# Output projection of three token blocks moved between in-projection blocks, operands split beside their weights, on one Trainium2 core

## The chip, the cores and the metric

The kernel runs on one core of a Trainium2 chip. The metric is the device time of one execution in microseconds (us). TensorE is called PE (its weight loads PEld), VectorE DVE, ScalarE ACT; SyncE (SP) issues every DMA of this kernel from one queue, in order. PE, DVE, ACT and SP each work through their own list of instructions in order; a framework writes these lists ahead of time, by a priority that follows the order of the Python program, and puts in the waits.

## The reference

One decoder layer over 2048 tokens of width 1024, in float32. What is computed, cut to its frame:

```
h = rmsnorm(x, norm1_w);  proj = h @ w_in                    # 1024 -> 3840
o_hg = hgrn2(first 2048 columns)                             # 4 heads of 128, gated linear recurrence
o_rw = rwkv7(last 1792 columns, shifted by a token and mixed)  # 8 heads of 64
x = x + concat(o_hg, o_rw) @ w_out
u = rmsnorm(x, norm2_w) @ w_up                               # 1024 -> 5632
u = causal depthwise conv of width 3 + bias;  gate, val = split(u)
x = x + (silu(gate) * val) @ w_down                          # 2816 -> 1024
out = rmsnorm(x, final_norm_w)
```

## The kernel before, in words

Tokens lie in four blocks (`nb` or `b`, 0 to 3) of 512. Every large product is made of three 128x512 matmuls a step (`mm3`, L194): each operand is split into a rounded high part, cast by ACT, and a low part, subtracted by DVE (`split`, L165, `split_to`, L161).

**Stage one** (`phase1`, L200) runs three generators side by side. `dense` (L343) is a list of jobs: for each block an "A" job (load four 128-token tiles of `x`, two at a time; square sum on ACT, scaling on DVE; transpose on PE, with ACT and DVE writing `hh` and `hl`), then 30 "P" jobs, each one 128-column strip of the in-projection: 24 matmuls into a `pj` bank, weights in `wraw` tiles (256 KB). At the end of the list stands "O" for block 0, `out_block` (L307): its output projection with the residual. `rw_stream` and `hg_stream` are the two recurrences, chains of small matmuls (`rw`, `hg` banks), DVE and ACT steps; the RWKV chain goes twice per pair of heads through DRAM (`Ed` to `E`, then `Td` to `TTs` and `TZ`). Each step of a recurrence lets `dense` proceed by 550 ns of matmuls (`fill`). There are two `pj` banks. Results go to DRAM: `oT` (recurrence outputs, transposed), `x1d` (residual rows), `h2d` (normalised, transposed rows for the next product).

**Output stage** (L926): for blocks 1, 2 and 3, one after another, load and split all eight `oT` tiles, load four `x` tiles, then for each half of the columns eight steps of twelve matmuls (`wacc`), add the residual, store `x1d`, and for blocks 1 and 2 normalise, transpose and store `h2d`. Then `build(0)`.

**Up-projection** (`half`, L984, for token halves 0 and 1): one level of a Strassen-like scheme, seven products in place of eight. `build(h)` (L898) makes its seven token operands: for each of four row groups `kk` it loads four 256 KB tiles of `h2d` (blocks 2h and 2h+1), forms sums with four DVE subtractions and splits seven tiles into `Bh`, `Bl`. For each of 22 feature blocks `fb`, weight tiles `uraw` are loaded, combined and split, and 84 matmuls go to `ua`, `ub`, `ud`; convolution and gate follow, and `gd` is stored to DRAM. Block 3 is normalised inside half 0 at `fb` 2 and 4 (`norm_last`, L968).

**Down-projection** (L1073): for each block load and split all 22 `gd` tiles (`graw`), then for each half of the columns 22 steps of a weight tile (`wdraw`) and twelve matmuls (`dacc`); residual, final norm, store.

Of the kernel before, what the change touches and what calls it, by code (L numbers as in the profile page):

```python
# [7 lines left out]
F32 = mybir.dt.float32  # L8
F32R = mybir.dt.float32r
BF16 = mybir.dt.bfloat16  # L10
# [8 lines left out]
P = 128  # L19
# [41 lines left out]
def tile_layer(ctx, tc, consts, x, norm1_w, w_in, hg_lb_logits, hg_norm_w, rw_shift_mu, rw_w0, rw_w2,  # L61
# [10 lines left out]

    cst = cp.tile([P, C_W], F32, name="cst")
    dma(cst, consts)
    ident = cst[:, C_ID:C_ID + P]
# [97 lines left out]
    def rstd(pool, xt, name, sqt="nsq"):  # L173

        sq = pool.tile([P, D], BF16, tag=sqt, name="nsq", bufs=1)
# [6 lines left out]
    def norm_transpose(pool, xt, nm, psum, evict, sqt="nsq"):  # L182

        n = len(xt)
        for t_ in xt:
            V.tensor_scalar_mul(t_, t_, rstd(pool, t_, "nst", sqt))
# [13 lines left out]
    def phase1(c1):  # L200
# [106 lines left out]
        def out_block(nb):  # L307

            for k in range(KD):
                raw = wp.tile([P, BLK], F32, tag="wraw", name="oraw", bufs=3)  # L310
                dma(raw, oT[nb][k * P:(k + 1) * P, :])
                split_to(hh[:, k, :], hl[:, k, :], raw)
            for i2 in range(2):
                xt = []
                for q in range(2):
                    t_ = wp.tile([P, D], F32, tag="xt", name="xt", bufs=2)
                    t0 = nb * BLK + (i2 * 2 + q) * P
                    dma(t_, x[0, t0:t0 + P, :])
                    xt.append(t_)
                for dh in range(2):  # L320
                    accs = [bank("pj") for _ in range(2)]
                    for k in range(KD):
                        raw = wp.tile([P, 512], F32, tag="wraw", name="woraw", bufs=3)
                        dma(raw, w_out[0, k * P:(k + 1) * P, dh * 512:dh * 512 + 512])
                        wh, wl = split(wp, raw, [P, 512], "w", 4)
                        for q in range(2):
# [3 lines left out]
                    for q in range(2):  # L330
                        V.tensor_add(xt[q][:, dh * 512:dh * 512 + 512], accs[q], xt[q][:, dh * 512:dh * 512 + 512])
                for q in range(2):
                    r0 = (i2 * 2 + q) * P
                    dma(x1d[nb][r0:r0 + P, :], xt[q])

                def evict(k, tp, w):
                    t_ = wp.tile([P, 256], F32, tag="h2", name="h2", bufs=2)
                    act(t_, tp, AF.Copy, scale=w)
                    dma(h2d[nb][k * P:(k + 1) * P, i2 * 256:i2 * 256 + 256], t_)

                yield from norm_transpose(wp, xt, "n2", lambda: bank("pj"), evict)
# [524 lines left out]
    if "1" in stages:  # L866
        with ExitStack() as c1:
            phase1(c1)
# [264 lines left out]
```

## Time and profile before

| | us |
|---|---|
| median of 3 runs (range) | 3017.43 (3015.49 to 3018.39) |
| the profiled execution | 3016.65 |
| its span, first to last instruction | 3014.9 |
| PE busy in it | 2779.6 (92%) |
| DVE busy | 1973.2 (65%) |
| ACT busy | 1423.3 (47%) |
| first in-projection matmul | at 41.0 |
| first `wacc` matmul | at 1402.2 |
| first `ua` matmul | at 1609.3 |
| first `dacc` matmul | at 2521.8 |

"Granted clock" or PEclk is the share of its full clock that PE was given. A row of waits reads: who waited, for whom, us in total, how often, longest. In a group, the mean of one instruction in ns stands ahead of the second bar, and behind it the idle time ahead of the instructions with what ended it. Durations of matmuls overlap, since they are pipelined; the distance of their starts is what each costs.

### The profile page before, as it was taken

How to read it: one execution, taken by the hardware profiler on the slowest of the kernel's cores; microseconds unless marked ns; L12 is line 12 of the kernel's file. 1: busy time of each engine (PE TensorE's matmuls, PEld its weight loads, DVE VectorE, ACT ScalarE, POOL GpSimd, SP SyncE). 2: the span in 40 equal slices, each digit the busy share in tenths (PEclk: the TensorE clock that was granted, in tenths of full speed). 3: DMA queues.
4: the chain of work that ended last, by engine and by line, in shares of the span. 5: the costliest groups of instructions: out<-in, count | busy, mean ns of one | idle time of the engine just before them, and what ended most of it. 6: DMA issues, size and time to landing. Idle time of an engine off the chain costs nothing.

```text
span 3014.9 us, 47475 instructions
## 1 busy us (share of the span) xinstructions
PE 2779.6 (92%) x18323; PEld 2201.0 (73%) x18323; DVE 1973.2 (65%) x3889; ACT 1423.3 (47%) x2390; POOL 0.2 (0%) x4
## 2 busy tenths in 40 slices
PE   5999899989998999987678899998999995999998
PEld 4777677767776777666557788886888874888887
DVE  4778668776877586853545687778777774445343
ACT  4545553655354454543434655555555543334332
POOL 0000000000000000000000000000000000000000
PEclk9999899999998999988889999998999997999999
DMA  3222222222313222246653322223222216456442
GB/s 119 71 66 67 76 77 73 67 80 64 89 55 79 74 65 76 68 127 197 210 174 108 121 83 84 84 88 101 84 84 84 84 56 213 158 173 223 143 154 97
DMA packets 361295, 316.47 MB, mean 105 GB/s; under 512 B 61303, under 2 KB 278637, under 8 KB 361069
## 3 DMA queue, kind: packets, MB, share of 16 engines
q1 hardware_dynamic: 361069, 313.44, 33.8%
q8 instruction: 144, 2.36, 0.3%
q14 instruction: 82, 0.67, 0.1%
HBM read 250.44 MB, written 62.91 MB: 104 GB/s over the span
## 4 chain that ended last, share of the span: by engine, by line
PE 79%; DVE 7%; ACT 6%; DMA 5%; issue 2%; SPq 1%; DVEq 0%; ACTq 0%
PE pj L196 8%; PE pj L197 7%; PE pj L198 7%; PE ua L196 5%; PE ua L197 5%; PE ua L198 5%; PE dacc L196 5%; PE dacc L197 5%; PE dacc L198 5%; PE ud L198 2%; PE ud L196 2%; PE ud L197 2%; PE hg L750 2%; PE ub L196 1%; PE ub L198 1%
## 5 line engine op out<-in xcount | busy, mean ns | idle before, releaser
L196 PE MATMUL pj<-hh,wh 128*128 128x512 f32 x960 | 420.1, 438 | 1.5 <-ACT wh L169 0.9
L197 PE MATMUL pj<-hl,wh 128*128 128x512 f32 x960 | 382.3, 398 | 0.0
L198 PE MATMUL pj<-hh,wl 128*128 128x512 f32 x960 | 380.6, 396 | 0.6 <-DVE wl L170 0.6
L169 ACT CAST wh<-wraw 128x512 fp32r<-128x512 f32 x240 | 146.6, 618 | 347.5 <-PE pj L197 295.4
L196 PE MATMUL dacc<-wdh,ggh 128*128 128x512 f32 x704 | 274.4, 391 | 36.9 <-ACT wdh L169 36.9
L196 PE MATMUL ua<-Bh,uwh 128*128 128x512 f32 x704 | 276.9, 393 | 19.6 <-ACT m L108 9.9
L197 PE MATMUL ua<-Bl,uwh 128*128 128x512 f32 x704 | 276.0, 392 | 9.6 <-DVE Bl L163 9.6
L198 PE MATMUL ua<-Bh,uwl 128*128 128x512 f32 x704 | 275.2, 391 | 0.0
L197 PE MATMUL dacc<-wdl,ggh 128*128 128x512 f32 x704 | 275.0, 391 | 0.0
L198 PE MATMUL dacc<-wdh,ggl 128*128 128x512 f32 x704 | 274.8, 390 | 0.0
L170 DVE TENSOR_TENSOR wl<-wraw,wh 128x512 fp32r<-128x512 f32 x240 | 162.4, 684 | 146.3 <-ACT wh L169 144.8
L170 DVE TENSOR_TENSOR wdl<-wdraw,wdh 128x512 fp32r<-128x512 f32 x176 | 120.9, 689 | 184.9 <-ACT wdh L169 184.8
L169 ACT CAST uwh<-uraw 128x512 fp32r<-128x512 f32 x220 | 136.1, 619 | 203.7 <-PE ua L197 86.1
L196 PEld LDWEIGHTS pj<-hh,wh 128*128 128x128 f32 x960 | 180.9, 188 | 64.6 <-issue 20.1
L197 PEld LDWEIGHTS pj<-hl,wh 128*128 128x128 f32 x960 | 181.4, 189 | 40.8 <-issue 12.0
L198 PEld LDWEIGHTS pj<-hh,wl 128*128 128x128 f32 x960 | 180.8, 188 | 41.5 <-DVE wl L170 1.4
L169 ACT CAST wdh<-wdraw 128x512 fp32r<-128x512 f32 x176 | 109.0, 619 | 204.9 <-PE dacc L198 178.0
L170 DVE TENSOR_TENSOR uwl<-uraw,uwh 128x512 fp32r<-128x512 f32 x220 | 147.3, 685 | 86.0 <-ACT uwh L169 84.8
L196 PEld LDWEIGHTS dacc<-wdh,ggh 128*128 128x128 f32 x704 | 132.7, 189 | 65.4 <-ACT wdh L169 38.2
L196 PEld LDWEIGHTS ua<-Bh,uwh 128*128 128x128 f32 x704 | 133.1, 189 | 51.4 <-ACT m L108 12.7
L197 PEld LDWEIGHTS ua<-Bl,uwh 128*128 128x128 f32 x704 | 133.3, 189 | 37.7 <-DVE Bl L163 10.3
L198 PEld LDWEIGHTS ua<-Bh,uwl 128*128 128x128 f32 x704 | 133.1, 189 | 27.9 <-DVE uwl L170 0.2
(263 smaller groups left out, 5622.5 us busy)
## 6 DMA issues: line engine op xcount, KB each, us to landing
wraw<-in_w_in_dram SPq DMA_DIRECT2D x240, 256.0 KB
uraw<-in_w_up_dram SPq DMA_DIRECT2D x176, 256.0 KB
wdraw<-in_w_down_dram SPq DMA_DIRECT2D x176, 256.0 KB
gd<-y SPq DMA_DIRECT2D x88, 256.0 KB
graw<-gd SPq DMA_DIRECT2D x88, 256.0 KB
woraw<-in_w_out_dram SPq DMA_DIRECT2D x80, 256.0 KB
xt<-in_x_dram SPq DMA_DIRECT2D x32, 512.0 KB
xt<-x1d SPq DMA_DIRECT2D x20, 512.0 KB
```

The costliest lines, as they stand in the source:

```text
L169: S.copy(hi, src)
L170: V.tensor_sub(lo, src, hi.bitcast(F32))
L196: TE.matmul(acc, lh, rh, start=first, stop=False, skip_group_check=skip)
L197: TE.matmul(acc, lh, rl, start=False, stop=False, skip_group_check=skip)
L198: TE.matmul(acc, ll, rh, start=False, stop=last, skip_group_check=skip)
L750: TE.matmul(lp[e * 64:e * 64 + 64, b * 64:b * 64 + 64], kt[:, t0:t0 + 64], qt[:, t0:t0 + 64], start=True, stop=True, tile_position=(0, e * ...
```

## The change

The job list of stage one becomes longer. "O" for blocks 0, 1 and 2 now stand in it: O(0) ahead of A(2), O(1) ahead of A(3), O(2) at the end. A new job "L" loads the next block's four `x` tiles and scales them, twenty jobs into the block before, so that "A" only transposes, now all four tiles into one bank. A new job "N" normalises a block's `x1d` rows, read back from DRAM, and writes `h2d`: N(0) and N(1) ten jobs into blocks 2 and 3, N(2) at the end. `out_block` loads and splits each `oT` tile beside the weight tile of the same step and takes residual rows in halves. The tags of scratch tiles are merged (`wraw` with four buffers now also holds squares, residual halves and `h2`).

In the output stage block 3 alone is left, its `oT` tiles also split beside the weights. The sums of the Strassen operands are formed by `sums`, stored to DRAM (`Ts`) and read back by `build`, which now goes operand by operand through six buffers; those of half 1 are formed at `fb` 6 to 9 of half 0. In the down-projection `graw` tiles are loaded and split beside `wdraw` tiles. The first block's `x` tiles are loaded ahead of the small parameters.

```diff
+    def load_rows(src, r0):
+        t_ = xp_.tile([P, D], F32, tag="xt", name="xt", bufs=4)
+        dma(t_, src[r0:r0 + P, :])
+        return t_
+
     cst = cp.tile([P, C_W], F32, name="cst")
+    first = [load_rows(x[0], i * P) for i in range(2)]
     dma(cst, consts)
+    first += [load_rows(x[0], i * P) for i in range(2, 4)]
...
         def out_block(nb):
 
-            for k in range(KD):
-                raw = wp.tile([P, BLK], F32, tag="wraw", name="oraw", bufs=3)
-                dma(raw, oT[nb][k * P:(k + 1) * P, :])
-                split_to(hh[:, k, :], hl[:, k, :], raw)
             for i2 in range(2):
...
                     for k in range(KD):
-                        raw = wp.tile([P, 512], F32, tag="wraw", name="woraw", bufs=3)
+                        if i2 == 0 and dh == 0:
+                            raw = wp.tile([P, BLK], F32, tag="wraw", name="oraw", bufs=4)
+                            dma(raw, oT[nb][k * P:(k + 1) * P, :])
+                            split_to(hh[:, k, :], hl[:, k, :], raw)
+                        raw = wp.tile([P, 512], F32, tag="wraw", name="woraw", bufs=4)
...
+        def normed(src, r0, xt=None):
+
+            xt = xt or [load_rows(src, r0 + i * P) for i in range(4)]
+            for t_ in xt:
+                V.tensor_scalar_mul(t_, t_, rstd(wp, t_, "nst", "wraw", 4))
+            return xt
...
-            jobs = []
+            jobs = [("L", 0)]
             for nb in range(NBLK):
+                if nb >= 2:
+                    jobs.append(("O", nb - 2))
                 jobs.append(("A", nb))
...
-            jobs.append(("O", 0))
+            jobs += [("O", 2), ("N", 2)]
+
+            at = [i for i, jb in enumerate(jobs) if jb[0] == "A"]
+            for nb in reversed(range(NBLK)):
+                if nb + 1 < NBLK:
+                    jobs.insert(at[nb] + 20, ("L", nb + 1))
+                if nb >= 2:
+                    jobs.insert(at[nb] + 10, ("N", nb - 2))
...
+                if jb[0] == "L":
+                    xt = normed(x[0], jb[1] * BLK, first if jb[1] == 0 else None)
+                    continue
                 if jb[0] == "A":
...
+                    yield from transposed(xt, "n1", lambda: bank("pj"), to_h)
+                    continue
+                if jb[0] == "N":
+                    yield from transposed(normed(x1d[jb[1]], 0), "n2", lambda: bank("pj"), to_h2(jb[1]))
                     continue
...
+        Ts = [[dp.tile([4, P, BLK], F32, name=f"Ts{h}{kk}") for kk in range(4)] for h in range(2)]
+
+        def raw_(src):
+            t_ = hr.tile([P, BLK], F32, tag="br", name="br", bufs=6)
+            if src is not None:
+                dma(t_, src)
+            return t_
...
+        def sums(h, kk):
+
+            b11, b12, b21, b22 = (raw_(hsrc(h, q, b, kk)) for q in range(2) for b in range(2))
+            t1, t2 = raw_(None), raw_(None)
+            V.tensor_sub(t1, b12, b11)
+            V.tensor_sub(b12, b22, b12)
+            V.tensor_sub(t2, b22, t1)
+            V.tensor_sub(b21, b21, t2)
+            for i, t_ in enumerate((t1, t2, b12, b21)):
+                dma(Ts[h][kk][i], t_)
+
         def build(h):
 
...
+            for i, src in ((0, (0, 0)), (1, (1, 0)), (4, 1), (3, 0), (5, 2), (6, 3), (2, (1, 1))):
+                for kk in range(4):
+                    t_ = raw_(Ts[h][kk][src] if isinstance(src, int) else hsrc(h, *src, kk))
+                    split_to(Bh[i][:, kk, :], Bl[i][:, kk, :], t_)
...
+                    if h == 0 and 6 <= fb < 10:
+                        sums(1, fb - 6)
...
             for dh in range(2):
                 accs = [pst("dacc") for _ in range(4)]
                 for k in range(NFF):
-                    raw = dn.tile([P, 512], F32, tag="wdraw", name="wdraw", bufs=3)
+                    if dh == 0:
+                        raw = dn.tile([P, BLK], F32, tag="graw", name="graw", bufs=4)
+                        dma(raw, gd_[b][k * P:(k + 1) * P, :])
+                        ghl.append(split(dn, raw, [P, BLK], "gg", 24))
```

Three places show where instructions now stand. The first is PE at the boundary from block 1 to block 2, before; a row is number, line, operation, output and operands, shape. `pj<-cst,xt` are transposes of `x`, `hg` and `rw` rows belong to the recurrences.

```order
1812 L816 MATMUL hg<-osq,ones 128x512
1813 L190 MATMUL pj<-cst,xt 128x128 x4
1814 L740 MATMUL hg<-cst,hv 128x128 x4
1815 L190 MATMUL pj<-cst,xt 128x128 x8
1816 L609 MATMUL rw<-TZ_6424,M_5837 32x32 x16
```

The same boundary now. `pj<-wh,hh` and its two fellows are the output projection of block 0, `pj<-hh,wh` the in-projection of block 2.

```order
2044 L206 MATMUL pj<-wh,hl 128x512
2045 L205 MATMUL pj<-wl,hh 128x512
2046 L206 MATMUL pj<-wh,hl 128x512
2047 L198 MATMUL pj<-cst,xt 128x128 x32
2048 L204 MATMUL pj<-hh,wh 128x512
2049 L205 MATMUL pj<-hl,wh 128x512
2050 L206 MATMUL pj<-hh,wl 128x512
```

The recurrences' rows have moved up between the matmuls of the output projection, whose last 78 stand alone; the 32 transposes stand in one piece, and 192 in-projection matmuls follow them without a row of the recurrences (195 at the next boundary).

The second place is SP at the end of the output stage, before: the four residual stores of block 3, then the first weights of the up-projection (`uraw`).

```order
302 L951 DMA x1d_116<-xt_15427 128x1024
303 L951 DMA x1d_116<-xt_15429 128x1024
304 L951 DMA x1d_116<-xt_15431 128x1024
305 L951 DMA x1d_116<-xt_15433 128x1024
306 L993 DMA uraw<-in_w_up_dram 128x4x128 x6
```

Now, from the third of these stores; `br` are the tiles from which the token operands are split, `Ts` the stored sums.

```order
389 L970 DMA x1d_127<-xt_15487 128x1024
390 L970 DMA x1d_127<-xt_15488 128x1024
391 L921 DMA br<-h2d_128 128x512
392 L921 DMA br<-Ts_15474 128x512
...
407 L921 DMA br<-Ts_15477 128x512
408 L921 DMA br<-h2d_129 128x512 x4
409 L1006 DMA uraw<-in_w_up_dram 128x4x128 x6
```

Eighteen operand loads of the first half have come between the last store and the first weights; before, all operand loads of the half stood ahead of the stores.

The third place is SP at the entry to the down-projection, before and then now.

```order
477 L1075 DMA fw<-in_final_norm_w_dram 128x1024
478 L1080 DMA graw<-gd_121 128x512 x3
479 L1085 DMA xt_23110<-x1d_113 128x1024
480 L1080 DMA graw<-gd_121 128x512 x3
481 L1085 DMA xt_23112<-x1d_113 128x1024
```

```order
615 L1090 DMA fw<-in_final_norm_w_dram 128x1024
616 L1099 DMA graw<-gd_132 128x512
617 L1107 DMA wdraw<-in_w_down_dram 128x512
618 L1099 DMA graw<-gd_132 128x512
619 L1107 DMA wdraw<-in_w_down_dram 128x512
```

Token tiles and weight tiles now alternate from the first; the residual rows have moved behind the eighth step.

164 lines of the change are left out of this document (62 added, 102 removed).

## The prediction

> **What bounds the kernel now.** I read the page first, then cut the span into its stages with the busy time by windows, then asked for waits, chain and timeline in the stages that fall short. The page: TensorE (PE) is busy for 92% of the span, and for 79% of the chain that ended last.
>
> ```profile
> span 3014.9 us, 47475 instructions
> PE 2779.6 (92%) x18323; PEld 2201.0 (73%) x18323; DVE 1973.2 (65%) x3889; ACT 1423.3 (47%) x2390; POOL 0.2 (0%) x4
> PE 79%; DVE 7%; ACT 6%; DMA 5%; issue 2%; SPq 1%; DVEq 0%; ACTq 0%
> ```
>
> So a shorter time must come from the 235 us in which PE is idle and from the stretches at a low granted clock. The windows (start:end, length, busy time of PE, its weight loads, DVE, ACT, POOL, then granted clock, DMA share, GB/s) show where these lie:
>
> ```profile
> 0.00:41.00 41.00, 9.84 (x33) 4.89 (x34) 18.55 (x54) 18.29 (x39) 0.20 (x4) 1.00 0.41 128
> 300.00:350.00 50.00, 37.30 (x508) 29.55 (x506) 33.87 (x89) 23.00 (x54) 0.00 (x0) 0.73 0.25 67
> 350.00:625.00 275.00, 273.22 (x2395) 207.45 (x2394) 201.73 (x495) 141.57 (x235) 0.00 (x0) 1.00 0.26 72
> 625.00:675.00 50.00, 39.05 (x546) 30.49 (x544) 30.22 (x80) 30.14 (x67) 0.00 (x0) 0.86 0.34 94
> 950.00:1000.00 50.00, 39.27 (x573) 30.84 (x575) 27.91 (x74) 23.56 (x56) 0.00 (x0) 0.80 0.32 88
> 1275.00:1300.00 25.00, 14.01 (x159) 10.18 (x158) 12.87 (x28) 10.96 (x21) 0.00 (x0) 0.59 0.62 167
> 1350.00:1403.00 53.00, 33.85 (x136) 24.07 (x135) 23.79 (x40) 25.41 (x50) 0.00 (x0) 0.82 0.81 265
> 1403.00:1609.00 206.00, 149.53 (x639) 122.80 (x638) 88.49 (x140) 75.71 (x139) 0.00 (x0) 0.85 0.50 167
> 2040.00:2080.00 40.00, 27.21 (x92) 18.82 (x91) 38.13 (x63) 22.84 (x38) 0.00 (x0) 0.79 0.35 112
> 2080.00:2484.00 404.00, 403.31 (x1779) 333.48 (x1778) 309.04 (x440) 203.36 (x293) 0.00 (x0) 1.00 0.25 80
> 2484.00:2522.00 38.00, 1.51 (x7) 0.97 (x5) 17.16 (x22) 13.98 (x21) 0.00 (x0) 0.58 0.62 207
> ```
>
> Inside a block of the first stage (350 to 625) and inside the up-projection (2080 to 2484) PE is full. The holes are the start, the three block boundaries, the tail of the first stage (1275 to 1403), the separate output projection of blocks 1 to 3 (1403 to 1609), the second building of operands (2040) and the entry to the down-projection (2484). The last row but one gives the price of a 128x512 matmul: 404/1779 = 0.227 us.
>
> **The change part by part.** *Start.* PE waits here for normalised rows (waits, first 42 us):
>
> ```profile
> PE pj L190 <- DVE xt L186: 17.9, 4, 7.1
> ```
>
> Four tiles now come first, 2.1 MB with 0.75 MB of constants: 10 us at the 0.27 MB/us of the DMA rows further down. The small vectors land behind them, and on DVE the order puts memsets, constants and two weight splits ahead of the four scalings (0.75 us each, below). Then eight transposed groups follow, 1.1 us or more each (next part). In-projection starts near 32 instead of 41 us: **-9** (-18 if DVE is ready, +3 if the vectors come late).
>
> *Boundaries.* What a group costs follows from these groups of the output stage, of the page and of DVE as a whole (mean ns ahead of the second bar) and one row of the timeline (start, us):
>
> ```profile
> L108 ACT ACTIVATE h<-tp,vt 128x512 f32<-128x512 f32 x16 | 10.6, 685 | 21.5 <-DMA h2d<-h 15.5 <-PE tp L190 5.7 <-ACT h L108 0.3
> L186 DVE TENSOR_SCALAR xt<-xt,nst 128x1024 f32<-128x1024 f32 x8 | 6.0, 754 | 6.3 <-DMA x1d<-xt 5.8 <-ACT nst L108 0.5
> L170 DVE TENSOR_TENSOR wl<-wraw,wh 128x512 fp32r<-128x512 f32 x240 | 162.4, 684 | 146.3 <-ACT wh L169 144.8
> L298 DVE SCALAR_TENSOR_TENSOR hgg<-pj,vt,sgm 128x512 f32<-128x512 f32 x16 | 11.8, 738 | 1.1 <-ACT sgm L108 1.1
> 1452.98 5.11 PE L190 MATMUL tp<-cst,xt 128*128 128x128 f32 x32 [4.25 <-DVE xt L186]
> ```
>
> A bank passes four transposes (0.64), ACT (0.69) and DVE (0.74): 2.1 us, two banks, 1.07 a group, 8.6 us a boundary, of which 5.1 is PE's own work. The three boundary rows hold 12.7 + 11.0 + 10.7 = 34.4 us idle and, as busy time times missing clock, 10.1 + 5.5 + 7.9 = 23.5 us, together 58. Of it 3 x 3.5 stays, and some 15 for waits of the recurrences: **-32** (-50 to -10). I keep 6 of the 23.5 for half-speed matmuls. The Trainium skill (TensorE: Matmul & The Clock Gate, Part 1) halves the clock only after about 3.4 us without work; by that rule the 6 would go too and the sum be 6 lower. The timeline below agrees with its length: 0.43 us steps from 1609.3 to 1612.9.
>
> *Work moved in.* Blocks 0 and 1 now project inside stage one: 2 x 192 x 0.227 = 87 us of PE that nothing can hide, as PE is full there. Their normalisations add 2 x 8.6 = 17. Added waits: during these projections two of the four split-weight pairs are held by the next in-projection column, and after each the order has 192 or more in-projection matmuls with no recurrence work between (the first place shown with the change), so the recurrences have less filler later. No row prices that: 0 if filled, 45 if every boundary keeps its old hole; I take 15, nearer to the full rows. Together **+119**.
>
> *Tail.* It begins with PE waiting on the recurrence's DRAM round trip:
>
> ```profile
> PE rw L609 <- DMA TZ<-Td: 9.7, 3, 7.1
> ```
>
> The order now has 30 projection matmuls (6.8 us) ahead of that wait, since token operands are split beside the weights. That takes nearly all of the 11.0 idle and 5.7 clock of 1275 to 1300: -15. In 1350 to 1403 19.2 us idle and 6.1 clock are lost, in part to a normalisation in the middle of the projection that is gone: -6. Against it, the last normalisation (job N of block 2) now reads its rows back from DRAM: a store and a load before the first transpose, twice the 4.5 us of the x1d store shown below: +9. **-12** (-25 to +10).
>
> *Output stage.* Now 206 us for three blocks. Its waits, then the chain at its end (start, us), then two timeline rows of the clock:
>
> ```profile
> PE wacc L196 <- ACT ooh L169: 38.6, 2, 20.0
> 1600.64 4.49 DMA x1d<-xt
> 1605.38 3.07 DMA uraw<-in_w_up_dram
> 1609.30 0.79 PE ua L196
> 1610.32 0.63 PE L198 MATMUL ua<-Bh,uwl 128*128 128x512 f32 x1
> 1612.88 0.42 PE L198 MATMUL ua<-Bh,uwl 128*128 128x512 f32 x1
> ```
>
> One block remains: 192 x 0.227 = 43.6 us. But operand sums go through DRAM now, and SP issues the first up-projection weights behind all operand loads (the second place). From the first `wacc` matmul to the first `ua` the queue moves 10 weight tiles, 15 loads and 16 stores for sums, 28 operand loads and 4 weight tiles of 0.26 MB, and 3.1 MB of rows: 22 MB. DMA in its fullest stretches:
>
> ```profile
> 1350.00:1400.00 50.00, 32.54 (x132) 23.03 (x130) 23.39 (x38) 24.46 (x48) 0.00 (x0) 0.84 0.82 271
> 1450.00:1475.00 25.00, 5.11 (x32) 4.88 (x32) 6.09 (x10) 11.18 (x24) 0.00 (x0) 0.69 0.81 289
> ```
>
> At 0.28 MB/us that is 78 us; I take 77, the queue being the bound. Ends: 60 (the rest hidden beside the matmuls) and 100 (sums in series, four steps of about 10 us). **-129** (-146 to -106). The Trainium skill (DMA: Bandwidth & Descriptors, Specifications) allows a core about 358 GB/s of HBM: by it 62 us and a sum 15 lower. No row of this case came near it, so the rows decide.
>
> *Up-projection.* Sums of the second half add 16 subtractions in four feature blocks. A feature block is 84 x 0.227 = 19.1 us of PE; DVE fills 309/404 of it, 14.6 us, plus 4 x 0.68 (a 128x512 DVE row above) = 17.3, which PE still covers. Their 32 DMAs stand between weight issues on SP: **+4** (0 to 12). In exchange the building at 2040 loses those subtractions. There DVE was full (38.1 of 40) and PE lost 12.8 idle and 5.7 clock: **-10** (-15 to 0). Next late there are 28 loads through six buffers.
>
> *Down-projection.* First operand split and first matmul (timeline):
>
> ```profile
> 2501.01 1.79 ACT L169 CAST ggh<-graw 128x512 fp32r<-128x512 f32 x3 [8.32 <-DMA graw<-gd]
> 2521.77 0.79 PE L196 MATMUL dacc<-wdh,ggh 128*128 128x512 f32 x1 [36.49 <-ACT wdh L169]
> ```
>
> With each token tile split beside its weight tile (the third place) PE starts after the first pair, near 2502.5: **-19** (-21 to -10). What is late next would be the pairs: 0.52 MB per 12 matmuls (2.7 us), 0.19 MB/us, below the 0.27 seen.
>
> Sum: -9 - 32 + 119 - 12 - 129 + 4 - 10 - 19 = **-88**. The profiled execution took 3016.65 us (span 3014.9 and 1.75 around it); from it 2928.7, and from the median 3017.43, 0.8 above it, 2929.4. I say 2929.
>
> **The rivals.** *Everything fills* (0.16): the added stalls are 0, the output stage comes to 62 and boundaries gain 45: 88 + 15 + 15 + 13 = -131, 2886. For it: 99% busy inside blocks. Against: DMA at its limit.
>
> *The moved projections keep their price* (0.15): in the output stage a block costs 206/3 = 69 us; if it does so inside stage one too, 138 instead of 119, and the boundaries gain nothing because the recurrences' own chain shows there: -88 + 19 + 32 = -37, 2980.
>
> *The sums come in series* (0.13): output stage 112 us, -53, 2964. For it: one SP queue, in which stores wait for DVE ahead of weight loads.
>
> *Slower, by the SP queue* (0.04): the recurrence's DRAM round trips, two for each of six pairs of heads in blocks 1 to 3, are issued from the queue that now also holds projection loads waiting for buffers. If each stood 10 us longer on PE, 120 - 88 = +32, 3049. It decides from 7.4 us a trip, as much again as the longest wait now (7.1). Against: most trips lie beside in-projection, whose queue hardly changes.
>
> That the change is not in effect has no room: the order shows the moved matmuls; 0.02 is left for no change by several mishaps, 3017.
>
> **How the numbers follow.** The forecast has 0.50. The range 2885 to 2982 takes in the first three rivals. About 0.2% (6 us) is what a measurement of this kernel tells from no change. Faster 0.94, same 0.02, slower 0.04.
>
> **What would show it.** Right: first in-projection matmul before 36 us; no window of 50 us in stage one under 0.9 clock; the last in-projection matmul near 1354, the first `wacc` near 1468; from first `wacc` to first `ua` 70 to 85 us with DMA near 0.28 MB/us; PE idle before the down-projection under 20 us. Wrong: PE waits on `TZ<-Td` over 30 us in sum, a first stage longer by over 110 us, or `woraw` waits inside the output stage.

## The result, and the profile after

The changed kernel takes **2987.6 us** (median of four runs, 2981.64 to 2989.88) where the kernel before takes 3017.91 in the same runs (3015.49 to 3020.3). The ratio is 0.9897, with a 95% interval of 0.9879 to 0.9914: faster by 1.0%, or 30 us, where 88 were forecast. 2987.6 lies above the range of 2885 to 2982.

The page of the profiled execution (2986.09 us):

```profile
span 2984.2 us, 47821 instructions
PE 2787.2 (93%) x18323; PEld 2203.3 (74%) x18323; DVE 1989.2 (67%) x3889; ACT 1429.3 (48%) x2380; POOL 0.2 (0%) x4
```

PE issues the same 18323 matmuls; its idle time went from 235 to 197 us. Where, shows in the distance between landmarks (first or last matmul of a kind in the two timelines):

| stretch | before, us | after, us | difference | forecast |
|---|---|---|---|---|
| to the first in-projection matmul | 41.0 | 32.9 | -8.1 | -9 |
| on to the last of block 1 (one boundary) | 586.9 | 575.9 | -10.9 | -10.7 |
| on to the last of block 2 (boundary, O(0), N(0)) | 319.5 | 392.8 | +73.3 | +48.8 |
| on to the last of block 3 (boundary, O(1), N(1)) | 322.8 | 397.8 | +75.0 | +48.8 |
| tail, to the first `wacc` | 132.1 | 129.2 | -2.9 | -12 |
| output stage, to the first `ua` | 207.1 | 74.7 | -132.4 | -129 |
| up-projection, to the last `ud` | 876.0 | 872.9 | -3.1 | -6 |
| on to the first `dacc` | 36.5 | 16.7 | -19.8 | -19 |
| down-projection and end | 493.1 | 491.3 | -1.8 | 0 |

(The forecast column lays the -32 of three boundaries and the +119 of the moved work over three and two stretches.) Six rows of nine came out within 4 us; the two blocks with moved work miss by 51 together, the tail by 9.

The stages of the changed kernel in windows (start:end, length, busy time of PE, its weight loads, DVE, ACT, POOL, then granted clock, DMA share, GB/s):

```profile
0.00:33.00 33.00, 9.04 (x34) 5.88 (x34) 16.27 (x44) 16.09 (x31) 0.20 (x4) 1.00 0.52 171
295.00:313.00 18.00, 11.32 (x67) 9.07 (x66) 14.77 (x38) 10.83 (x16) 0.00 (x0) 0.89 0.35 95
609.00:718.00 109.00, 95.82 (x967) 71.26 (x966) 67.09 (x157) 45.18 (x83) 0.00 (x0) 0.89 0.45 142
718.00:728.00 10.00, 6.00 (x36) 3.69 (x35) 7.65 (x11) 5.98 (x10) 0.00 (x0) 1.00 0.62 185
781.00:800.00 19.00, 11.68 (x56) 7.63 (x54) 14.85 (x27) 14.82 (x27) 0.00 (x0) 0.73 0.19 72
1177.00:1199.00 22.00, 15.37 (x56) 9.08 (x56) 14.81 (x27) 16.36 (x25) 0.00 (x0) 0.64 0.22 83
1504.00:1529.00 25.00, 8.62 (x35) 6.18 (x35) 7.29 (x13) 12.41 (x22) 0.00 (x0) 0.63 0.80 285
1529.00:1575.00 46.00, 46.00 (x192) 37.59 (x191) 22.51 (x37) 9.96 (x16) 0.00 (x0) 0.94 0.80 263
1575.00:1603.00 28.00, 0.16 (x1) 0.00 (x0) 20.00 (x34) 15.83 (x26) 0.00 (x0) 0.57 0.93 321
2040.00:2080.00 40.00, 28.92 (x119) 23.06 (x118) 32.31 (x51) 23.15 (x38) 0.00 (x0) 0.87 0.47 142
2476.00:2493.00 17.00, 0.27 (x2) 0.08 (x1) 6.94 (x8) 4.84 (x6) 0.00 (x0) 0.62 0.41 128
```

The boundaries (295, 718) are what was hoped: 18 and 10 us. But the projection O(0) takes 109 us (609 to 718), with 13 us idle and a clock of 0.89, and the normalisations N(0) and N(1) 19 and 21 us at clocks of 0.73 and 0.64. In the output stage the matmuls run without a hole (1529), and then PE stands for 28 us while DMA moves 321 GB/s.

Inside O(0), finer windows, then the longest of PE's waits (who, for whom, us in all, times, longest), of ACT's and of SP's from 609 to 718. A "raw" tile holds a loaded operand ahead of its split, a "split pair" its high and low part:

```profile
620.00:630.00 10.00, 7.74 (x83) 5.87 (x81) 7.27 (x16) 3.23 (x7) 0.00 (x0) 0.83 0.57 131
630.00:640.00 10.00, 5.23 (x89) 4.58 (x88) 6.92 (x19) 0.95 (x3) 0.00 (x0) 0.50 0.37 108
640.00:650.00 10.00, 10.00 (x143) 8.91 (x142) 4.14 (x10) 7.14 (x19) 0.00 (x0) 0.65 0.23 80
```

```profile
PE hg L767 <- DVE KTs L785: 3.8, 3, 1.3
PE pj L204 <- ACT wh L179: 3.8, 5, 1.7
```

```profile
ACT wh L179 <- DMA woraw<-in_w_out_dram: 14.1, 6, 3.8
ACT wh L179 <- PE pj L206: 13.4, 11, 2.3
...
ACT hh L172 <- DMA oraw<-oT: 5.2, 2, 3.1
```

```profile
SPq L323 <- DVE hl L173: 16.1, 3, 10.4
SPq L326 <- DVE wl L180: 14.7, 16, 2.4
SPq L332 <- DVE wl L180: 10.3, 6, 3.4
```

From 625 to 648 PE has only the recurrences' small matmuls; the three windows (0.83, 0.50, 0.65) put a clock of one half at about 626.6 to 647. Later PE waits for split weights (`wh`). ACT, which casts them, waits for their loads (14.1 us in six waits of up to 3.8) and nearly as long, 13.4 us, until PE is done with an older split pair. The loads themselves are issued late: SP waits for DVE's subtractions (`hl`, `wl`), the last users of a raw tile, before it can load the next one into it (L323 loads token tiles, L326 weight tiles, L332 residual rows). The wait on `TZ<-Td`, the sign of the slower rival, 17.5 us in the kernel before, is gone from the list of PE's waits.

### The profile page after: what moved, and what is told of

Its sections match the earlier page's. It is cut to its first block, busy times and chain, and to the rows that moved or that the text cites. A ratio compares the mean times of both kernels' runs of the same rounds, so it can differ in the third digit from the quotient of the medians.

```text
span 2984.2 us, 47821 instructions
## 1 busy us (share of the span) xinstructions
PE 2787.2 (93%) x18323; PEld 2203.3 (74%) x18323; DVE 1989.2 (67%) x3889; ACT 1429.3 (48%) x2380; POOL 0.2 (0%) x4
## 3 DMA queue, kind: packets, MB, share of 16 engines
q1 hardware_dynamic: 382957, 351.20, 37.6%
## 4 chain that ended last, share of the span: by engine, by line
PE 81%; ACT 7%; DVE 6%; DMA 4%; issue 2%; SPq 0%; DVEq 0%; ACTq 0%
PE pj L204 8%; PE pj L205 7%; PE pj L206 7%; PE dacc L204 5%; PE dacc L205 5%; PE dacc L206 5%; PE ua L204 5%; PE ua L205 5%; PE ua L206 5%; PE ud L205 3%; PE ud L206 3%; PE ud L204 3%; PE hg L767 2%; DMA woraw<-in_w_out_dram 1%; PE ub L204 1%
## 5 line engine op out<-in xcount | busy, mean ns | idle before, releaser
L204 PE MATMUL pj<-hh,wh 128*128 128x512 f32 x960 | 412.2, 429 | 3.0 <-ACT wh L179 1.9
L204 PE MATMUL dacc<-wdh,ggh 128*128 128x512 f32 x704 | 275.0, 391 | 16.7 <-ACT wdh L179 16.7
L204 PEld LDWEIGHTS dacc<-wdh,ggh 128*128 128x128 f32 x704 | 132.7, 188 | 44.6 <-ACT wdh L179 17.2
L205 PEld LDWEIGHTS dacc<-wdl,ggh 128*128 128x128 f32 x704 | 132.6, 188 | 28.1 <-DVE wdl L180 0.5
```

Source lines behind the costliest of these rows:

```text
L204: TE.matmul(acc, lh, rh, start=first, stop=False, skip_group_check=skip)
L205: TE.matmul(acc, lh, rl, start=False, stop=False, skip_group_check=skip)
```

## The experiments

Each ratio is against the kernel before on the same chip. Where two variants are compared, it is by their medians; the runs of one variant lie within 3 to 17 us, so differences of a few us between medians say little. Theory: the moved work is dear because of where it stands. Rival: it costs about what I forecast, and something else ate the gain.

### The two blocks put back

In stage one the jobs O(0), O(1), N(0), N(1) go. That leaves one block at the tail and three in the output stage, as many as in the kernel before. In the output stage:

```diff
-            b = NBLK - 1
-            ohl = []
...
+            for b in (0, 1, 3):
+                ohl = []
...
+                if b < 2:
+                    for t_ in xt:
+                        V.tensor_scalar_mul(t_, t_, rstd(hr, t_, "nst", "br", 6))
...
+                        t_ = hr.tile([P, BLK], F32, tag="br", name="h2", bufs=6)
...
+                    for _ in transposed(xt, "n2", lambda: pst("tp"), evict):
+                        pass
```

> The changed kernel with the output projection and normalisation of blocks 0 and 1 taken out of stage one and put back into the output stage (there with token operands split beside the weights); all the rest of the change stays. Theory A (the moved work is dear inside stage one): from the last in-projection matmul of block 1 to that of block 2 the changed kernel needs 392.6 us where the kernel before needs 319.5, and for block 3 397.8 against 322.8; without the moved work these stretches fall to about 309 and 312 (10.9 below the kernel before, as the first boundary did), 170 less in all; the output stage grows by two blocks of some 62, 125. Time about 2987 - 45 = 2942: moving the two blocks was a loss. Rival B (as I forecast, the moved work costs about 60 a block and the output stage 65 a block): about 2990, no difference. Rival C (without the moved matmuls the recurrences' waits come back at the two boundaries, 39 us each as before): 2987 - 148 + 125 = 2964.

Measured: **2938.22**, ratio 0.9736 (0.9719 to 0.9754). Moving blocks 0 and 1 into stage one cost 49 us. First two windows of the changed kernel, for blocks 2 and 3 of the in-projection with all that stands between; then those of this run, for the same blocks, for blocks 0 and 1 of the output stage, and for the wait ahead of `ua`:

```profile
609.00:1001.00 392.00, 363.34 (x3135) 275.83 (x3134) 267.11 (x627) 197.66 (x346) 0.00 (x0) 0.96 0.36 106
1001.00:1399.00 398.00, 372.03 (x3135) 279.57 (x3133) 265.57 (x626) 193.78 (x330) 0.00 (x0) 0.94 0.33 101
```

```profile
607.00:919.00 312.00, 302.96 (x2916) 231.37 (x2916) 233.28 (x577) 159.01 (x280) 0.00 (x0) 0.99 0.27 73
919.00:1232.00 313.00, 303.66 (x2908) 231.42 (x2906) 232.54 (x576) 154.31 (x264) 0.00 (x0) 0.99 0.24 67
1358.00:1413.00 55.00, 51.40 (x226) 42.51 (x227) 23.81 (x38) 20.46 (x42) 0.00 (x0) 0.93 0.50 171
1413.00:1466.00 53.00, 48.25 (x225) 39.97 (x224) 23.43 (x36) 25.78 (x51) 0.00 (x0) 0.99 0.68 237
1511.00:1525.00 14.00, 0.00 (x0) 0.00 (x0) 5.81 (x12) 1.79 (x3) 0.00 (x0) 0.67 0.97 348
```

A block of in-projection with its boundary takes 311.8 and 312.9 us, so the moved work had made them 80.9 and 84.9 longer; by the windows, PE was idle 36 us more in them and busy 129 us more. In the output stage the same work takes 55 and 53 us. Rivals B and C are out: the boundaries keep their gain (-7.6 and -9.9) with no projection to fill them. The 58 us between the two places do not all arrive, since the up-projection of this run takes 898.5 us, 26 more than in the changed kernel. Its output stage is not that of the kernel before: the normalised rows `h2` leave through `br` tiles, which matters further down.

### What makes them dear in stage one

**Held pairs.** The forecast's reason for stalls: the next column's weights, split early, hold two of four pairs.

```diff
-                load(i + 1)
+                if jobs[jn + 1][0] != "O":
+                    load(i + 1)
...
+                        if i2 == 1 and dh == 1 and k == KD - 1:
+                            late()
```

> The changed kernel with one thing put off: the weights of the in-projection column that follows an output projection in stage one are loaded and split at the end of that projection and not ahead of it, so that all four split pairs and all four raw tiles are free for the projection. Theory A (two of four pairs held is what starves these projections, as I forecast for 15 us): the idle time of 13.5 and 12.4 us in the two projections falls by half or more, 12 to 16 us less, about 2973. Rival B (the idle time there is the recurrences' own chain of DVE steps and DRAM round trips): less than 6 us.

Measured 2982.97, ratio 0.9883 (0.9862 to 0.9903): 4.6 less than the changed kernel, where the theory asked for 12 to 16. The projections take 106.3, 101.6 and 103.4 us in place of 109.1, 108.2 and 104.1. Held pairs are a small part.

**Changes of kind.** A moved matmul occupies PE for 0.28 to 0.30 us on average (the distance to the next start, idle time taken off), in part at half clock, and not for 0.227.

```diff
                         for q in range(2):
                             ...
-                            yield 680
+                        yield 1360
```

> The changed kernel with the output projections inside stage one given out six matmuls at a time instead of three, so that PE changes about half as often between them and the recurrences' small matmuls. Theory A (a change of kind is what makes a moved matmul cost 0.286 us on average where 0.227 was reckoned): the mean falls to about 0.26, 576 matmuls times 0.025, 14 us less, about 2973. Rival B (the price is the wait for split weights or the clock in these stretches, not the changes): no difference, 2987 +- 5. Rival C (larger portions leave the recurrences waiting longer between two of their steps): 5 to 15 slower.

Measured 2983.9, ratio 0.9889 (0.9873 to 0.9906). This 3.7 us is within the scatter. It tells little: the framework re-ordered, and in O(0) PE still goes from projection to recurrence 24 times where it went 29 times.

**The normalisations' wait.**

```diff
+                    jobs.insert(at[nb] + 4, ("M", nb - 2))
...
+                if jb[0] == "M":
+                    xm = normed(x1d[jb[1]], 0)
+                    continue
```

> The changed kernel with the normalisation of blocks 0 and 1 inside stage one cut in two: rows are read back and scaled six jobs earlier than they are transposed, as is done for the in-projection's rows. Theory: the transposes' wait for scaled rows (25.3 us in all, longest 10.2) is what makes the two N jobs cost 18.9 and 21.2 us instead of 8.6; with the rows ready they fall to about 10 each and the clock stays at 1.00 there: 18 to 22 us less, about 2967. Rival: PE is late for another reason at these two places (the recurrence's own waits, 2.7 and 3.6 us of idle there), and the time moves by less than 6.

Measured 2975.81, ratio 0.9861 (0.9846 to 0.9877), 11.8 less. N(0) falls from 18.9 to 14.1 us and N(1) from 21.1 to 15.1. PE's waits there, first of the changed kernel, then of this one:

```profile
PE pj L198 <- DVE xt L346: 4.4, 1, 4.4
PE rw L496 <- DVE BV L494: 2.9, 2, 2.7
```

```profile
PE pj L198 <- ACT h L118: 3.4, 1, 3.4
PE rw L501 <- DVE BV L499: 0.5, 1, 0.5
```

The wait for scaled rows is gone; one for ACT's evictions stands in its place, so that only half of the 22.8 us above 2 x 8.6 came back: less than the theory's 18 to 22, more than the rival's 6.

**The stream of tiles.** Three of four weight tiles left out; then three of four token tiles as well; then the loads alone, with every split kept.

```diff
+                        if k % 4 == 0:
                             raw = wp.tile([P, 512], F32, tag="wraw", name="woraw", bufs=4)
                             dma(raw, w_out[0, k * P:(k + 1) * P, dh * 512:dh * 512 + 512])
                             wh, wl = split(wp, raw, [P, 512], "w", 4)
```

> The changed kernel with three of four weight tiles of the output projections in stage one left out: every fourth row group's split pair is used for four row groups, so the product of blocks 0 to 2 is not the reference's; the matmuls, the token operands and all the rest stay. Theory A (the stream of weights, a load, a cast and a subtraction for every six matmuls, is what leaves PE idle and at a low clock in these projections): each falls from 109, 108 and 104 us by 12 or more, 2950 or less. Rival B (the recurrences' own chain, which drains in these stretches, sets their length): less than 4 us each, 2978 or more.

> As the run with few weight tiles, and three of four token-operand tiles of those projections left out too (their place in the operand buffers keeps the in-projection's rows), so the product of blocks 0 to 2 is not the reference's. Theory A (the first quarter of each projection, with a token tile and a weight tile for six matmuls, is where PE runs the recurrences alone at 0.5 to 0.7 of its clock; the loads make that hole): the projections fall from 98.8, 96.2 and 93.9 us by 8 or more each, 2925 or less. Rival B (the recurrences' chain leaves that hole): less than 3 us each, 2940 or more.

> As the run with few weight and token tiles, but only the loads are left out: each of the four row groups is cast and subtracted again, from the tile that was loaded for the first of them (the product of blocks 0 to 2 is not the reference's). With neither loads nor splits the projections took 90.6, 90.3 and 88.8 us and the kernel 2924.8, with both 109.1, 108.2 and 104.1 and 2987.6. Theory A (the loads, and the queue they come through, set the pace): 94 or less each, 2935. Rival B (the splits, which stand among the recurrences' steps in the lists of ScalarE and VectorE, set it): 104 or more, 2972 or above.

Measured: 2947.02 (ratio 0.9765, 0.9747 to 0.9783), 2924.82 (0.9687, 0.9667 to 0.9707) and 2950.19 (0.9778, 0.9752 to 0.9803). The three projections took:

| | O(0) | O(1) | O(2) | kernel |
|---|---|---|---|---|
| changed kernel | 109.1 | 108.2 | 104.1 | 2987.6 |
| few weight tiles | 98.8 | 96.2 | 93.9 | 2947.0 |
| few weight and token tiles | 90.6 | 90.3 | 88.8 | 2924.8 |
| the same, all splits kept | 94.2 | 97.7 | 93.7 | 2950.2 |

Three quarters of the stream cost 18.5 + 17.9 + 15.3 = 51.7 us: 35.9 by the loads (first row less the last), 15.8 by the splits. Each time the theory came nearer than its rival, though most projections fell a few us short of what it asked (10.3, 12.0 and 10.3 for 12, then 8.2, 5.9 and 5.0 for 8; 97.7 for 94). (A further 7 of the differences between medians are in the wait ahead of the first `ua`, 28.1 in the changed kernel and 20.5 to 21.2 in these three; that was not followed up.) O(0) without the stream, then with the splits alone:

```profile
609.00:700.00 91.00, 87.02 (x966) 67.14 (x964) 49.73 (x129) 27.59 (x54) 0.00 (x0) 0.98 0.29 89
```

```profile
610.00:704.00 94.00, 86.64 (x963) 64.33 (x960) 66.12 (x157) 42.94 (x79) 0.00 (x0) 1.00 0.27 81
```

The clock is back at 0.98 and 1.00. So most of the hole from 625 to 648 in the changed kernel came from missing tiles for the projection, and not from the recurrences' own chain.

**Which part of the loads.** First another queue, then one raw tile fewer.

```diff
-                            dma(raw, oT[nb][k * P:(k + 1) * P, :])
+                            nc.gpsimd.dma_start(raw, oT[nb][k * P:(k + 1) * P, :])
...
-                        dma(raw, w_out[0, k * P:(k + 1) * P, dh * 512:dh * 512 + 512])
+                        nc.gpsimd.dma_start(raw, w_out[0, k * P:(k + 1) * P, dh * 512:dh * 512 + 512])
```

> The changed kernel with the loads of token and weight tiles of the output projections in stage one issued from GpSimd's queue and no longer from SyncE's, which also holds the recurrences' round trips, stores and the in-projection's loads. Theory A (the loads stand in line: SyncE waited 16.1 us for free token tiles and 14.7 for free weight tiles in the first projection, with everything else of stage one behind): the three projections fall by 8 or more each, 2962 or less. Rival B (the four raw tiles, or the casts and subtractions behind the loads, set the pace, whichever queue issues): less than 4 each, 2976 or more.

Measured 2995.59, ratio 0.9923 (0.9905 to 0.9942); projections 109.0, 108.4 and 113.0. The line in SyncE's queue is not the reason: in O(0) GpSimd, which here has these loads alone to issue, itself stood 43.2 us, in twelve waits, until a subtraction (`wl`) had freed a raw tile.

```diff
-                        raw = wp.tile([P, 512], F32, tag="wraw", name="woraw", bufs=4)
+                        raw = wp.tile([P, 512], F32, tag="wraw", name="woraw", bufs=3)
```

(and so for every tile of the tag `wraw`)

> The changed kernel with three raw tiles in stage one in place of four, as the kernel before had; all else stays. Theory A (the turn-around of the raw tiles sets the pace of the moved projections: a tile is taken from the issue of its load to the end of its subtraction, and two of them hold residual rows near each end of a half): each of the three projections grows by 6 to 15, the in-projection columns, with two tiles for 24 matmuls, stay as they were: 3005 to 3030. Rival B (the number of tiles does not matter, the loads are late for another reason): less than 3 each, 2987 +- 6.

Measured 3014.18, ratio 0.9983 (0.9969 to 0.9997); projections 118.1, 115.9 and 124.1, in-projection as before (block 3 behind N(1): 198.7, in the changed kernel 200.7). O(0) of this run, and PE's wait for split weights in it (3.8 us with four tiles):

```profile
608.00:727.00 119.00, 101.05 (x961) 72.54 (x962) 67.48 (x156) 44.31 (x81) 0.00 (x0) 0.87 0.41 131
```

```profile
PE pj L204 <- ACT wh L179: 12.2, 8, 2.8
```

One tile fewer adds 36.7 us over the three (O(2) alone 20.0, more than the 15 expected), as much as three quarters of the loads cost with four. With the waits of SP and GpSimd for freed tiles, this shows that the turn-around of the raw tiles, from the issue of a load to the end of its subtraction, sets the pace here. More than four tiles were not tried, so what more would bring is open.

### What made a block dear in the output stage before

In the kernel before, the loop over eight `oraw` tiles ahead of a block's weights goes, the residual rows are loaded at its steps 4 to 7, and in the weight loop:

```diff
+                        if dh == 0:
+                            raw = op_.tile([P, BLK], F32, tag="oraw", name="oraw", bufs=2)
+                            dma(raw, oT[b][k * P:(k + 1) * P, :])
+                            ohl.append(split(op_, raw, [P, BLK], "oo", 8))
```

> The kernel before with one part of the change alone: in its output stage (blocks 1 to 3) the token operands are loaded and split beside the weight tiles of the same step, no block is moved. Theory A (what made a block of that stage cost 69 us was the wait for all eight split token tiles, 38.6 us in two waits, not the place of the projection): a block falls to about 55 as in the run with the two blocks put back, 2 x 15 for blocks 2 and 3 and a few us at the first, 35 less: 2983, as much as the whole change brought. Rival (the loads are only put off, PE then waits tile by tile): less than 10 gained, 3008 or more.

Measured 3019.96, ratio 0.9992 (0.9979 to 1.0006): no effect, and the wait is still there:

```profile
PE wacc L196 <- ACT ooh L169: 37.9, 2, 19.8
```

Theory A was wrong. SyncE's list in the kernel before, after block 1, shows what the splits wait for (start, time, issue):

```profile
1458.08 0.90 SPq L956 DMA_DIRECT2D h2d<-h  x2
...
1462.45 1.05 SPq L956 DMA_DIRECT2D h2d<-h  x2
...
1467.50 0.97 SPq L956 DMA_DIRECT2D h2d<-h  x2
...
1471.91 0.90 SPq L956 DMA_DIRECT2D h2d<-h  x2
1474.61 1.00 SPq L931 DMA_DIRECT2D oraw<-oT  x2
```

The eight `h2d` stores go two by two, 4.4 to 5.1 us apart, and only then come the next block's token tiles: both use the two tiles of the tag `oraw`. One line gives `h2` others:

```diff
-                    t_ = op_.tile([P, BLK], F32, tag="oraw", name="h2", bufs=2)
+                    t_ = hr.tile([P, BLK], F32, tag=f"br{k % 2}{k // 2 % 2}", name="h2", bufs=1)
```

> The kernel before with one line changed: in its output stage the normalised tiles on their way to DRAM go through the four tiles of the operand builder and no longer through the two tiles into which the next block's token operands are loaded. Theory (the 37.9 us that PE waits there, unchanged when token operands were only split beside the weights, are the queue of eight stores through two shared tiles, behind which the next block's loads stand): the two waits of 20.0 and 18.6 us fall to a few us, 25 to 35 us less, about 2988. Rival (the loads themselves, 2.1 MB of token tiles and 2.1 MB of rows a block, are the wait): less than 8 us.

Measured **2981.01**, ratio 0.9872 (0.9853 to 0.989). One line in the kernel before brings at least what the whole change brings (37.6 us for 30.3), and a little more than the 25 to 35 expected. Its output stage takes 165.6 us in place of 207.1, and of PE's waits there `ooh` is gone. The longest now are:

```profile
PE ua L196 <- DMA uraw<-in_w_up_dram: 12.2, 1, 12.2
PE tp L190 <- DVE xt L186: 7.1, 3, 3.5
```

### Sums through DRAM, and the mends together

`build_direct` loads the sixteen `h2d` tiles of half 0 and forms its operands on chip, as before; half 1 keeps `Ts`.

```diff
-            for kk in range(4):
-                sums(0, kk)
-            build(0)
+            build_direct(0)
```

> The changed kernel with the operands of the first half formed on chip as before (16 tiles loaded, four subtractions and seven splits for each of four row groups) and not by way of DRAM; the second half keeps its sums in DRAM. Theory (the output stage's end is bound by what its one queue has to move): 16 stores and 12 loads of 0.26 MB less, 7.3 MB or 26 us at the 0.28 MB/us seen; the 28.1 us between the last wacc matmul and the first ua matmul fall to about 10, as in the kernel before (9.4): 2970. Rival (DVE, which then has some 53 us of splits, sums and residual work beside 46 us of matmuls, takes the queue's place): 2980 or no gain.

Measured 2965.82, ratio 0.9832 (0.9809 to 0.9855), 21.8 less than the changed kernel; the wait ahead of `ua` is 10.4 us in place of 28.1, as expected. So the queue bounded the end of that stage, and DVE did not take its place.

The next adds to this the rows read ahead, and block 2 normalised in half 0:

```diff
-            jobs += [("O", 2), ("N", 2)]
+            jobs += [("O", 2)]
...
-                    if h == 0 and fb in (2, 4):
-                        norm_last(fb // 2 - 1)
+                    if h == 0 and fb in (1, 2, 4, 5):
+                        norm_last(2 + fb // 4, int(fb in (2, 5)))
```

> The changed kernel with the three mends together and the blocks left where the change put them: normalisation of blocks 0 and 1 read and scaled six jobs ahead, operands of the first half formed on chip, block 2 normalised in the up-projection. Theory (place and mends add up): from 2987.6, 11.8 and 21.8 as measured apart, 12 for the tail's normalisation: 2942. With the two blocks put back the same tail of mends gave 2902, so that the place alone would then cost 40 and not the 49 of the first comparison. Rival (the mends overlap, since all of them unload the one queue at the same place): 2955.

Measured 2945.36, ratio 0.9761 (0.9744 to 0.9777): the mends add up, nearly. And the same with the two blocks put back (the first diff of this section), for which no rows need reading ahead:

> A version made from what the first runs showed: the changed kernel with blocks 0 and 1 projected and normalised in the output stage, the first half's operands formed on chip without DRAM sums, and block 2 normalised inside the first half of the up-projection, as block 3 is. From the 2938 of the run with the two blocks put back: its up-projection lost 30.4 us of idle time and some 8 of clock in its first 175 us and 14.6 us ahead of the first ua matmul, of which about 10 stay: -40; the tail's normalisation (18.6 us and the 4.5 behind it) goes, about 10 come back in the up-projection: -13. About 2887. Rival (DVE is the bound in forming the operands at the end): 2910 to 2925.

Measured **2902.16**, ratio 0.9613 (0.9594 to 0.9631), the fastest version: 3.9% below the kernel before. Against the run above, the place of two blocks costs 43 us. The 15 us short of 2887 are in the up-projection, which takes 889.1 us and in the changed kernel 872.9. Its first half now holds the transposes of two blocks, and PE is idle there for 15.3 us in place of 9.6; whether the normalisations cause these waits was not tested (two rows of windows, start of half 0):

```profile
1525.00:1550.00 25.00, 20.45 (x85) 16.70 (x84) 13.62 (x22) 14.25 (x26) 0.00 (x0) 0.86 0.42 137
1550.00:1575.00 25.00, 22.62 (x107) 18.05 (x106) 18.50 (x28) 18.80 (x32) 0.00 (x0) 1.00 0.44 147
```

Last, from this version block 2's projection also goes to the output stage:

```diff
-            jobs += [("O", 2)]
...
-            for b in (0, 1, 3):
+            for b in range(NBLK):
```

> The best version so far (blocks 0, 1 and 3 projected in the output stage) with block 2 put back as well, so that no projection is left in stage one. Theory (a projection pays in stage one only where the in-projection has run out and PE would be idle): behind the last in-projection matmul the recurrences of block 3 drain alone, 37.5 us of their matmuls at a low clock and the waits of their chain, 65 to 80 us in place of the 102 with the projection; the output stage grows by 53. Time 2902 + 25 = about 2927. Rival (the projection costs as much there as elsewhere in stage one, 27 more than in the output stage): 2902 or below.

Measured 2905.36, ratio 0.9625 (0.961 to 0.964). The tail falls from 103.1 to 65.3 us, as expected, but the output stage grows by 45 and not 53, which I had taken from blocks with a normalisation behind them. At the tail, where the in-projection has run out, the projection costs 37.8 us net, 7 less than in the output stage by these two profiled executions. The medians differ by 3.2 us only and the intervals overlap, so that it pays there is not shown: the two places cost about the same. The theory had the kernel 25 us slower without it, the rival no slower at all.

## Why the forecast was wrong, point by point

**Start, boundaries, output stage, up- and down-projection: right in size.** Start -8.1 for -9; the three boundaries -10.9, -7.6 and -9.9 (the last two from the run with the blocks put back), together -28 for -32; output stage -132 for -129; up-projection -3 for -6; down-projection -20 for -19. Three of these were partly luck. The boundaries' terms (58 us lost, of which 10.5 and 15 stay) give 32 only if nothing is kept for half-speed matmuls; with the 6 that I named they give 26. In the up-projection the second building gave some 4 of its 10 us (between 2040 and 2080 idle 12.8 to 11.1, clock 5.7 to 3.8), and the sums cost next to nothing in place of 4. In the output stage the queue was to be the bound throughout, but in the first 46 us PE's own matmuls ran without a hole. (Between the last store and the first weights stand 21 operand loads and not 18, since the last row of that list is four.)

**Work moved in: the step that failed.** It said: "Added waits: during these projections two of the four split-weight pairs are held by the next in-projection column ... No row prices that: 0 if filled, 45 if every boundary keeps its old hole; I take 15". Measured against the run with the blocks put back, the moved work is 80.9 + 84.9 = 166 us, not 119. Less the 87 us of matmuls and the 17 of normalisation, as they were reckoned, 62 us are added waits and low clock, four times the 15 and beyond the upper bound of 45. The reason named for them was a small one: free pairs brought under 5 us. What the runs showed in its place is 37 us for three quarters of the stream of tiles (blocks 2 and 3 take 392.8 and 397.8 us with it, 375.7 and 377.6 with few tiles), and 11 us in N(0) and N(1) for rows that were not read ahead. The other 14 us have no experiment of their own. Up to 12 of them lie in N(0) and N(1) (18.9 + 21.1 - 17.2 - 10.8), but recurrence matmuls run in these windows too, which would be done elsewhere without them.

The reason for the stream's cost stood in the code beside the one that I named. An in-projection column needs two raw tiles for 24 matmuls, `out_block` one for six, and in its first quarter two for six, all through the same four. I priced the matmuls and left out the tiles' turn-around, from load to subtraction.

**Tail.** -3 for -12. From the last in-projection matmul to the end of the projection it takes 103.9 us and took 114.2, so -10 for the -21 forecast; the normalisation behind it adds 7 for 9. The stream of tiles may be the reason here too, since O(2) is 15.3 us shorter without three quarters of it, but the projection at the tail of the kernel before had a stream as well, so this is argued and not shown.

**The gain was partly borrowed.** The output stage's -129 was right in size, but it took for the price of a block there 69 us, in which each of two gaps between blocks held about 20 us of waiting for two shared tiles. The row for it stood in the prediction (21.5 us idle, 15.5 of it "<-DMA h2d<-h"), and I read only the mean duration from it. With own tiles a block costs 53 to 55 us, 81 to 85 in stage one; seen so, the move could not pay. That -129 came out is thus no proof that the move was good: 41 us of it (207.1 to 165.6) could be had by one line.

**Rivals.** "Everything fills" failed at once, with 62 us of added waits. "The moved projections keep their price" came near by its number (2980), but by luck, as both halves of it failed: the price was 166 and not 138, and the boundaries did gain. The sums did not come in series (74.7 us, not 112; the prediction itself gives 100 for that case in another place). The wait on `TZ<-Td` did not grow, it went. Of the signs of being right, the start, the 74.7 us and the wait ahead of the down-projection came true; a window of stage one under a clock of 0.9 (109 us at 0.89), the last in-projection matmul at 1399 for 1354 and the first `wacc` at 1529 for 1468 did not. One sign of being wrong came true: the first stage is 126 us longer, over 110.

**The rate of DMA.** It moved 321 GB/s over 28 us here and 348 over 14 us in the run with the blocks put back, more than the 280 that I took for its limit. The 358 GB/s of the Trainium skill (DMA: Bandwidth & Descriptors, Specifications) was nearer. The stage still took 74.7 us and not 62, since its first 46 ran at 263.

## What to carry to other kernels

Before moving work into a stage that is full, count per matmul what each shared tile buffer must turn over there, and compare it with the work it displaces: by PE time alone this move looked like a gain, and the tiles made it a loss. Ask of the place it leaves why it was dear there; a wait between two uses of one small buffer may be cured by one line, after which the move has nothing to win. Test the parts of a bundled change one by one: here moving blocks 0 and 1 cost 49 us, and the rest earned 80 (3018.0 to 2938.2). By the profiled executions of these two, the rest is 40 us in the output stage, where the tiles of `h2` changed as well, 30 in the boundaries and the blocks between them, 20 at the entry to the down-projection, 8 at the start and 6 at the tail, against 22 lost in the up-projection.

## What the runs showed of the hardware

The granted clock was 0.50 from about 626.6 to 647 us though PE was never idle for long. PE's rows around the fall and behind it in the changed kernel (start, length, instruction; idle time ahead in brackets):

```profile
626.39 0.30 PE L767 MATMUL hg<-hq,hk 128*64 128x64 f32 x2 [1.52 <-DVE hk L752]
...
630.95 1.12 PE L767 MATMUL hg<-QTs,KTs 128*64 128x64 f32 x16 [0.94 <-DVE QTs L781]
633.35 1.12 PE L767 MATMUL hg<-QTs,KTs 128*64 128x64 f32 x16 [1.28 <-DVE KTs L785]
635.75 0.87 PE L767 MATMUL hg<-QTs,KTs 128*64 128x64 f32 x10 [1.28 <-DVE KTs L785]
```

The longest gap is 1.52 us, right ahead of the fall. The Trainium skill (TensorE: Matmul & The Clock Gate, Part 1) gives a window of about 3.4 us without work for the fall to half clock. Here short gaps were enough: the 3.4 us from 623.2 to 626.6 still hold 1.4 us of matmuls. The whole trace of the changed kernel says the same. In it the clock falls 18 times after the start; cut into steps of 3.41 us that line up with the falls, PE was busy for at most 0.48 of the step ahead of each, and where the clock stayed full, for at least 0.47 (in the kernel before 0.57 and 0.47, so the bound is not sharp). So in these kernels idle time alone understates what such a stretch costs: what counts is how much of some 3.4 us PE was at work.
